# Row-wise argmax on one core: groups of four tiles, matching on GpSimd, five load buffers and a transposed result

## The chip, the core and the metric

The kernel runs on one core of a Trainium2 chip. A core has a matrix engine (TensorE, PE), VectorE (DVE), ScalarE (ACT), GpSimd (POOL) and SyncE (SP), which here only issues DMAs. Each engine works through its own instructions in order and they meet at semaphores. On-chip memory (SBUF) has 128 partitions; data comes from device memory over 16 DMA engines that all queues share. The metric is the device time of one execution in microseconds (us); lower is better.

## The reference

```python
def setup_inputs():
    return {"x": np.random.randn(8192, 8192).astype(np.float32)}

def reference(x):
    return np.argmax(x, axis=1)
```

For each of 8192 rows of 8192 floats, the position of the first maximum, as int64. The input is 268 MB and is read once in full; the output is 64 KB.

## The kernel before

The rows are worked in 64 tiles of 128 rows, one row per partition, so a tile is 4 MB. Each row is seen as C = 64 chunks of L = 128 elements. One loop over the tiles does all of the following for a tile before the next:

1. SP loads the tile into `xt` (L38).
2. VectorE reduces each chunk to its maximum, `chunkmax`, 128x64 (L41), the one instruction that reads the whole tile.
3. VectorE takes the eight largest of these (MAX8, L45; the row's maximum is the first) and the position of the maximum among the chunks, `cidx` (FIND_INDEX8, L46, with a load of the value to match ahead of it).
4. VectorE makes of it the number of the chunk in the input seen as (8192 x 64) chunks, `idx_full` (L49, L50).
5. POOL issues an indirect DMA, the gather (L54): it fetches for each row the one chunk that holds the maximum from device memory again, into `ga`, 128x128.
6. VectorE finds the maximum's position in that chunk, `lidx` (L62), and adds `cidx` x 128 (L67, L69) into the low word of `o`, whose high word ACT has cleared (L65).
7. SP stores `o`, 8 bytes per row (L71).

All tiles of SBUF come from pools with three buffers, so `xt` has three. The order on each engine is that of the loop: VectorE goes on to the next tile's reduce (L41) only after it has waited for this tile's gather at L62 and written `o` at L69. SP has one queue of issues with loads and stores in it: a load behind a store can be issued only when that store's wait for `o` is over. Index work on L67 doesn't need the gather and stands ahead of L62.

Of the kernel before, what the change touches and what calls it, by code (L numbers as in the profile page):

```python
# [1 line left out]

# [4 lines left out]


@with_exitstack
def kernel(  # L10
    ctx: ExitStack,
    tc: tile.TileContext,
    x: bass.AP,
    out: bass.AP,
):
    nc = tc.nc
    N, M = x.shape
    P = 128
    C = 64
    L = M // C  # L20
    ntiles = N // P

    pool = ctx.enter_context(tc.tile_pool(name="argmax_sbuf", bufs=3))
    opool = ctx.enter_context(tc.tile_pool(name="argmax_out", bufs=3))

    oth = out.tensor
    oth2 = type(oth)(name=oth.name, shape=[N, 2], dtype=mybir.dt.int32, base_partition=oth.base_partition)
    out_u32 = oth2.ap()

    x_flat = x.tensor.reshape([N * C, L]).ap()  # L30

    cpool = ctx.enter_context(tc.tile_pool(name="argmax_const", bufs=1))
    rowbase = cpool.tile([P, 1], mybir.dt.uint32)
    nc.gpsimd.iota(out=rowbase, pattern=[[1, 1]], base=0, channel_multiplier=C)  # L34

    for t in range(ntiles):
        xt = pool.tile([P, M], x.dtype)
        nc.sync.dma_start(out=xt[:, :], in_=x[t * P:(t + 1) * P, :])  # L38

        chunkmax = opool.tile([P, C], x.dtype)  # L40
        nc.vector.reduce_max(out=chunkmax, in_=xt.rearrange("p (c l) -> p c l", c=C), axis=mybir.AxisListType.X)  # L41

        mx8 = opool.tile([P, 8], x.dtype)
        cidx = opool.tile([P, 8], mybir.dt.uint32)
        nc.vector.max(out=mx8, in_=chunkmax)  # L45
        nc.vector.max_index(out=cidx, in_max=mx8, in_values=chunkmax)  # L46

        idx_full = opool.tile([P, 1], mybir.dt.uint32)
        nc.vector.tensor_tensor(out=idx_full, in0=cidx[:, 0:1], in1=rowbase, op=mybir.AluOpType.add)  # L49
        nc.vector.tensor_scalar(out=idx_full, in0=idx_full, scalar1=t * P * C, scalar2=None,  # L50
                                op0=mybir.AluOpType.add)

        ga = pool.tile([P, L], x.dtype)
        nc.gpsimd.indirect_dma_start(  # L54
            out=ga[:, :],
            out_offset=None,
            in_=x_flat[:, :],
            in_offset=bass.IndirectOffsetOnAxis(ap=idx_full[:, :1], axis=0),
        )

        lidx = opool.tile([P, 8], mybir.dt.uint32)
        nc.vector.max_index(out=lidx, in_max=mx8, in_values=ga)  # L62

        o = opool.tile([P, 2], mybir.dt.int32)
        nc.scalar.memzero(o[:, 1:2])  # L65
        tmp = opool.tile([P, 1], mybir.dt.uint32)
        nc.vector.tensor_scalar(out=tmp, in0=cidx[:, 0:1], scalar1=L, scalar2=None,  # L67
                                op0=mybir.AluOpType.mult)
        nc.vector.tensor_tensor(out=o[:, 0:1], in0=tmp, in1=lidx[:, 0:1], op=mybir.AluOpType.add)  # L69

        nc.sync.dma_start(out=out_u32[t * P:(t + 1) * P, :], in_=o[:, :])  # L71


# [1 line left out]
_INS = ['x']  # L75
_OUTS = [((8192,), 'int64')]


# [23 lines left out]
```

## Time and profile before

| | us |
|---|---|
| time, median of 3 runs | 1073.86 (1071.63 to 1075.15) |
| profiled execution: span from the first to the last instruction (no other time of it is recorded) | 1087.8 |
| VectorE busy | 639.6 |
| GpSimd busy | 60.8 |
| ScalarE busy | 14.0 |

The profile is of one execution of its own, under the hardware profiler, and its span is longer than the three timed runs. Its page has groups of instructions: line, engine, operation, the tiles written and read with their shapes, the count, then the busy time in us and the mean of one in ns, then the idle time of the engine just before these instructions and what ended that idle time. The 40 slices of the span show how evenly the work is spread. Digits are the busy share in tenths:

```profile
DVE  3657556465574664655656557556465574655756
POOL 0000000000000000000000000000000000000000
DMA  9888877787788777878787787887787878778760
GB/s 404 237 294 234 251 293 213 263 263 227 294 237 248 277 217 275 256 234 293 216 272 256 217 294 234 256 288 199 277 259 230 294 216 272 263 209 294 239 231 5
```

The first slice, when three loads are queued at the start, moves 404 GB/s; the others some 200 to 300. DMA share is the mean busy share of the 16 DMA engines.

### The profile page before, as it was taken

How to read it: one execution, taken by the hardware profiler on the slowest of the kernel's cores; microseconds unless marked ns; L12 is line 12 of the kernel's file. 1: busy time of each engine (PE TensorE's matmuls, PEld its weight loads, DVE VectorE, ACT ScalarE, POOL GpSimd, SP SyncE). 2: the span in 40 equal slices, each digit the busy share in tenths (PEclk: the TensorE clock that was granted, in tenths of full speed). 3: DMA queues.
4: the chain of work that ended last, by engine and by line, in shares of the span. 5: the costliest groups of instructions: out<-in, count | busy, mean ns of one | idle time of the engine just before them, and what ended most of it. 6: DMA issues, size and time to landing. Idle time of an engine off the chain costs nothing. (4 is left out here: it accounts for less than half of the span.)

```text
span 1087.8 us, 1198 instructions
## 1 busy us (share of the span) xinstructions
DVE 639.6 (59%) x640; ACT 14.0 (1%) x65; POOL 60.8 (6%) x69
## 2 busy tenths in 40 slices
DVE  3657556465574664655656557556465574655756
ACT  0000000000000000000000000000000000000000
POOL 0000000000000000000000000000000000000000
DMA  9888877787788777878787787887787878778760
GB/s 404 237 294 234 251 293 213 263 263 227 294 237 248 277 217 275 256 234 293 216 272 256 217 294 234 256 288 199 277 259 230 294 216 272 263 209 294 239 231 5
DMA packets 20489, 272.78 MB, mean 251 GB/s; under 512 B 11264, under 2 KB 11264, under 8 KB 12288
## 3 DMA queue, kind: packets, MB, share of 16 engines
q1 hardware_dynamic: 18432, 268.51, 76.6%
q0 software_dynamic: 2048, 4.20, 1.0%
q14 instruction: 9, 0.07, 0.0%
HBM read 272.63 MB, written 0.07 MB: 251 GB/s over the span
## 5 line engine op out<-in xcount | busy, mean ns | idle before, releaser
L41 DVE TENSOR_REDUCE chunkmax<-xt 128x64 f32<-128x8192 f32 x64 | 555.5, 8679 | 13.3 <-DMA xt<-in_x_dram 13.0
L62 DVE MATCH_VALUE_LOAD lidx<-mx,ga 128x8 f32 x64 | 5.9, 92 | 417.9 <-DMA ga<-in_x_dram,idx_full 417.9
L54 POOL DMA_INDIRECT ga<-in_x_dram,idx_full x64 | 60.5, 945 | 1019.4 <-DVE idx_full L50 1019.4
L65 ACT ACTIVATE o<-o 128x1 uint32<-128x1 uint32 x64 | 12.8, 202 | 1030.8 <-DMA out_dram<-o 1030.8
L62 DVE FIND_INDEX8 lidx<-mx,ga 128x8 uint32<-128x128 f32 x64 | 18.2, 285 | 0.0
L45 DVE MAX8 mx<-chunkmax 128x8 f32<-128x64 f32 x64 | 14.6, 228 | 2.2
L46 DVE FIND_INDEX8 cidx<-mx,chunkmax 128x8 uint32<-128x64 f32 x64 | 14.0, 219 | 0.0
L69 DVE TENSOR_TENSOR o<-tmp,lidx 128x1 int32<-128x1 uint32 x64 | 10.2, 159 | 6.0 <-issue 0.4
L49 DVE CUSTOM_DVE_ANT_0 idx_full<-cidx,rowbase 128x2 uint16<-128x2 uint16 x64 | 10.2, 159 | 2.3
L50 DVE TENSOR_SCALAR idx_full<-idx_full 128x1 uint32<-128x1 uint32 x64 | 9.8, 153 | 0.0
L67 DVE TENSOR_SCALAR tmp<-cidx 128x1 uint32<-128x1 uint32 x64 | 9.4, 147 | 0.0
L46 DVE MATCH_VALUE_LOAD cidx<-mx,chunkmax 128x8 f32 x64 | 5.9, 92 | 2.2
L65 ACT ACT_TABLE_LOAD x1 | 1.3, 1283 | 0.7 <-PEq L86 0.7
L34 POOL IOTA rowbase<- 128x1 uint32 x1 | 0.1, 118 | 0.4 <-PEq L97 0.4
L86 POOL MEMSET const-uint8-127<- 128x1 uint8 x1 | 0.1, 118 | 0.0
L86 POOL MEMSET const-bfloat16-1.0<- 128x1 bf16 x1 | 0.1, 113 | 0.0
L86 POOL MEMSET const-float32-0.0<- 128x1 f32 x1 | 0.1, 98 | 0.2 <-issue 0.2
L86 POOL MEMSET const-float32-1.0<- 128x1 f32 x1 | 0.1, 104 | 0.0
## 6 DMA issues: line engine op xcount, KB each, us to landing
xt<-in_x_dram SPq DMA_DIRECT2D x64, 4096.0 KB, 15.8
ga<-in_x_dram,idx_full POOLq DMA_INDIRECT x64, 6.3
out_dram<-o SPq DMA_DIRECT2D x64, 1.0 KB, 3.7
```

The source lines that it names most:

```text
L34: nc.gpsimd.iota(out=rowbase, pattern=[[1, 1]], base=0, channel_multiplier=C)
L41: nc.vector.reduce_max(out=chunkmax, in_=xt.rearrange("p (c l) -> p c l", c=C), axis=mybir.AxisListType.X)
L45: nc.vector.max(out=mx8, in_=chunkmax)
L46: nc.vector.max_index(out=cidx, in_max=mx8, in_values=chunkmax)
L49: nc.vector.tensor_tensor(out=idx_full, in0=cidx[:, 0:1], in1=rowbase, op=mybir.AluOpType.add)
L50: nc.vector.tensor_scalar(out=idx_full, in0=idx_full, scalar1=t * P * C, scalar2=None, op0=mybir.AluOpType.add)
L54: nc.gpsimd.indirect_dma_start(out=ga[:, :], out_offset=None, in_=x_flat[:, :], in_offset=bass.IndirectOffsetOnAxis(ap=idx_full[:, :1], ax ...
L62: nc.vector.max_index(out=lidx, in_max=mx8, in_values=ga)
L65: nc.scalar.memzero(o[:, 1:2])
L67: nc.vector.tensor_scalar(out=tmp, in0=cidx[:, 0:1], scalar1=L, scalar2=None, op0=mybir.AluOpType.mult)
L69: nc.vector.tensor_tensor(out=o[:, 0:1], in0=tmp, in1=lidx[:, 0:1], op=mybir.AluOpType.add)
L86: nc = _bacc.Bacc("TRN2", target_bir_lowering=False, num_devices=1)
```

## The change

The loop is rewritten. What it does now:

- **Loads.** `xt` has five buffers, and SP's queue holds nothing but loads until the end. The last tile is loaded in four parts and reduced in four.
- **Groups.** Tiles go in groups, fifteen of four, then two, one and one. The chunk maxima of a group lie in one tile `cm`, and one VectorE reduce (L93) gives the row maxima `mx` of the whole group.
- **Matching.** MAX8 and FIND_INDEX8 are gone. `first_match` does on POOL, per tile, an is-equal with the row's maximum and a product with descending weights (n, n-1, ..., 1); the largest product, taken by a VectorE reduce, tells the first match. It is used for the chunk (64 values) and, after the gather, within the chunk (128 values).
- **Stages.** After a group's last tile comes stage 2 (`mx`, matches of the chunks); one tile later stage 3 (`k`, `idx`, the group's gathers, matches in the chunks); three tiles after that stage 4 (`k2` and the result `res`). The list `pending` holds what is due. The calls wrapped in `keep` stay in the order in which they are written.
- **Result.** `res` holds one column per tile in float32. TensorE transposes 60 columns, and at the end the last four, against an identity matrix; ACT copies them as integers into the low words of `o`, whose high words were cleared by a POOL memset; SP stores whole rows of 128 results. There are two stores in place of 64.

The diff, cut to its core; the old loop, printed above, is removed whole:

```diff
-    pool = ctx.enter_context(tc.tile_pool(name="argmax_sbuf", bufs=3))
-    opool = ctx.enter_context(tc.tile_pool(name="argmax_out", bufs=3))
+    xpool = ctx.enter_context(tc.tile_pool(name="x_sbuf", bufs=5))
+    spool = ctx.enter_context(tc.tile_pool(name="small", bufs=3))
+    cpool = ctx.enter_context(tc.tile_pool(name="const", bufs=1))
+    ppool = ctx.enter_context(tc.tile_pool(name="psum", bufs=2, space=bass.MemoryType.PSUM))
...
+    descC = cpool.tile([P, C], F32)
+    nc.gpsimd.iota(out=descC, pattern=[[-1, C]], base=C, channel_multiplier=0,
+                   allow_small_or_imprecise_dtypes=True)
...
+    def first_match(vals, mx, desc, n, g, name):
+
+        w = spool.tile([P, g, n], F32, tag=f"w_{name}")
+        for i in range(g):
+            keep(nc.gpsimd.tensor_scalar(out=w[:, i, :], in0=vals[:, i, :], scalar1=mx[:, i:i + 1],
+                                    scalar2=None, op0=ALU.is_equal))
+            keep(nc.gpsimd.tensor_tensor(out=w[:, i, :], in0=w[:, i, :], in1=desc, op=ALU.mult))
+        k = spool.tile([P, g], F32, tag=f"k_{name}")
+        return w, k
+
+    groups = [4] * 15 + [2, 1, 1]
...
+    def run_due(now, all_=False):
+        while pending and (all_ or pending[0][0] <= now):
+            pending.pop(0)[1]()
+
+    def defer(due, fn):
+        pending.append((due, fn))
+        pending.sort(key=lambda e: e[0])
+
+    def store(t0, n):
+        ps = ppool.tile([n, P], F32, tag="ps")
+        nc.tensor.transpose(ps, res[:, t0:t0 + n], ident)
+        o = spool.tile([n, P, 2], I32, tag="o")
+        nc.gpsimd.memset(o, 0)
+        nc.scalar.copy(out=o[:, :, 0:1], in_=ps.unsqueeze(2))
+        keep(nc.sync.dma_start(out=out_i32[t0:t0 + n, :], in_=o.rearrange("t p two -> t (p two)")))
+
+    def stage2(t0, g, cm, now):
+        mx = spool.tile([P, g], F32, tag="mx")
+        keep(nc.vector.reduce_max(out=mx, in_=cm, axis=AX.X))
+        w, k = first_match(cm, mx, descC, C, g, "c")
+
+        def stage3():
+            keep(nc.vector.reduce_max(out=k, in_=w, axis=AX.X))
+            idx = spool.tile([P, g], U32, tag="idx")
+            keep(nc.vector.tensor_tensor(out=idx, in0=base[:, t0:t0 + g], in1=k, op=ALU.subtract))
+            ga = spool.tile([P, g, L], F32, tag="ga")
+            for i in range(g):
+                keep(nc.gpsimd.indirect_dma_start(
+                    out=ga[:, i, :], out_offset=None, in_=x_flat[:, :],
+                    in_offset=bass.IndirectOffsetOnAxis(ap=idx[:, i:i + 1], axis=0)))
+            w2, k2 = first_match(ga, mx, descL, L, g, "l")
+
+            def stage4():
+                keep(nc.vector.reduce_max(out=k2, in_=w2, axis=AX.X))
+
+                keep(nc.vector.scalar_tensor_tensor(out=res[:, t0:t0 + g], in0=k, scalar=float(L),
+                                               in1=k2, op0=ALU.mult, op1=ALU.add))
...
+                if t0 + g == 60:
+                    store(0, 60)
+
+            defer(now + 4, stage4)
+
+        defer(now + 1, stage3)
...
+            xt = xpool.tile([P, M], F32, tag="xt")
+            parts = 4 if t == NT - 1 else 1
+            w = M // parts
+            cw = C // parts
+            for q in range(parts):
+                keep(nc.sync.dma_start(out=xt[:, q * w:(q + 1) * w],
+                                  in_=x[t * P:(t + 1) * P, q * w:(q + 1) * w]))
+            for q in range(parts):
+                keep(nc.vector.reduce_max(
+                    out=cm[:, i, q * cw:(q + 1) * cw],
+                    in_=xt[:, q * w:(q + 1) * w].rearrange("p (c l) -> p c l", c=cw), axis=AX.X))
+            run_due(t)
+            t += 1
+        now = t - 1
+        stage2(t0, g, cm, now)
+    run_due(0, all_=True)
+    while pending:
+        run_due(0, all_=True)
+    store(60, NT - 60)
```

How this moves instructions on three engines. On VectorE, before, the second tile (DMAHW is the semaphore of a load, DMASW that of a gather, DVE and Pool those of the engines):

```order
L41 TENSOR_REDUCE chunkmax<-xt 128x64 [waits DMAHW1_49]
L45 MAX mx_91<-chunkmax 128x8 [waits DVE_49]
L46 MAX_INDEX cidx<-mx_91,chunkmax 128x8 [waits DVE_49]
L49 ISA idx_full<-cidx,rowbase 128x2 [waits DVE_49]
L67 TENSOR_SCALAR tmp<-cidx 128x1
L50 TENSOR_SCALAR idx_full<-idx_full 128x1 [waits DVE_49]
L62 MAX_INDEX lidx<-mx_91,ga 128x8 [waits DMASW1_49]
L69 TENSOR_TENSOR o<-tmp,lidx 128x1 [waits DVE_49]
```

On VectorE, changed, from stage 4 of the first group (after tile 7's reduce) to the reduce of tile 10 (`k<-w` at L108 is `k2` of the text, taken from the matches within the chunks; at L97 it is `k`, from the matches of the chunks):

```order
L108 TENSOR_REDUCE k<-w 128x4 [waits Pool_49]
L110 SCALAR_TENSOR_TENSOR res<-k 128x4 [waits DVE_49]
L112 TENSOR_SCALAR res<-res 128x4 [waits DVE_49]
L93 TENSOR_REDUCE mx<-cm 128x4
L135 TENSOR_REDUCE cm<-xt 128x64 [waits DMAHW0_49]
L97 TENSOR_REDUCE k<-w 128x4 [waits Pool_49]
L99 TENSOR_TENSOR idx<-base,k 128x4 [waits DVE_49]
L135 TENSOR_REDUCE cm<-xt 128x64 [waits DMAHW1_49]
L135 TENSOR_REDUCE cm<-xt 128x64 [waits DMAHW2_49]
```

VectorE's wait for a gather is gone; it waits for POOL twice a group instead, with a reduce or three between the cause and the wait.

On SP, before, from the start of the program:

```order
L38 DMA xt<-in_x_dram 128x8192 x3
L71 DMA out_dram<-o 128x2 [waits DVE_49,Activation_49]
L38 DMA xt<-in_x_dram 128x8192 [waits DMAHW0_49]
L71 DMA out_dram<-o 128x2 [waits DVE_49,Activation_49]
L38 DMA xt<-in_x_dram 128x8192 [waits DMAHW1_49]
```

On SP, changed, all of the program, without the waits (each load from the sixth on waits for the reduce that last read its buffer):

```order
L171 UNCONDITIONAL_BRANCH
L132 DMA xt<-in_x_dram 128x8192 x63
L132 DMA xt<-in_x_dram 128x2048 x4
L89 DMA out_dram<-o 60x256
L89 DMA out_dram<-o 4x256
```

Between two loads there stood a store that waited for the tile's result; now no store stands ahead of any load.

On POOL, changed, at the end of the program (the chunk matches, gather and in-chunk matches of tile 62, then of tile 63; before, POOL had only the 64 gathers):

```order
L63 TENSOR_SCALAR w<-cm,mx 128x64 [waits DVE_49]
L65 TENSOR_TENSOR w<-w,descC 128x64 [waits Pool_49]
L102 DMA ga<-in_x_dram,idx 128x128 [waits DVE_49]
L63 TENSOR_SCALAR w<-ga,mx 128x128 [waits DMASW6_49]
L65 TENSOR_TENSOR w<-w,descL 128x128 [waits Pool_49]
L63 TENSOR_SCALAR w<-cm,mx 128x64 [waits DVE_49]
L65 TENSOR_TENSOR w<-w,descC 128x64 [waits Pool_49]
L102 DMA ga<-in_x_dram,idx 128x128 [waits DVE_49]
L63 TENSOR_SCALAR w<-ga,mx 128x128 [waits DMASW7_49]
L65 TENSOR_TENSOR w<-w,descL 128x128 [waits Pool_49]
```

POOL's matches of tile 63's chunks now stand behind its wait for the gather of tile 62.

More of the change, by code (lines that the diff above doesn't have):

```diff
@@ L6 @@
 from concourse._compat import with_exitstack
+F32 = mybir.dt.float32
+U32 = mybir.dt.uint32
+I32 = mybir.dt.int32
+ALU = mybir.AluOpType
+AX = mybir.AxisListType
 @with_exitstack
@@ L28 @@
-    out_u32 = oth2.ap()
+    oth2 = type(oth)(name=oth.name, shape=[NT, 2 * P], dtype=I32, base_partition=oth.base_partition)
+    out_i32 = oth2.ap()
     x_flat = x.tensor.reshape([N * C, L]).ap()
[L32 to L71, printed above, removed]
@@ new lines @@
+    descC = cpool.tile([P, C], F32)
+    nc.gpsimd.iota(out=descC, pattern=[[-1, C]], base=C, channel_multiplier=0,
+                   allow_small_or_imprecise_dtypes=True)
+    descL = cpool.tile([P, L], F32)
+    nc.gpsimd.iota(out=descL, pattern=[[-1, L]], base=L, channel_multiplier=0,
+                   allow_small_or_imprecise_dtypes=True)
+    base = cpool.tile([P, NT], F32)
+    nc.gpsimd.iota(out=base, pattern=[[P * C, NT]], base=C, channel_multiplier=C,
+                   allow_small_or_imprecise_dtypes=True)
@@ new lines @@
+    ident = cpool.tile([P, P], F32)
+    nc.gpsimd.iota(out=ident, pattern=[[1, P]], base=0, channel_multiplier=-1,
+                   allow_small_or_imprecise_dtypes=True)
+    keep(nc.gpsimd.tensor_scalar(out=ident, in0=ident, scalar1=0.0, scalar2=None, op0=ALU.is_equal))
+    res = cpool.tile([P, NT], F32)
+    def first_match(vals, mx, desc, n, g, name):
[6 more added lines that the diff above has]
+        return w, k
@@ new lines @@
+    groups = [4] * 15 + [2, 1, 1]
+    assert sum(groups) == NT
+    pending = []
+    def run_due(now, all_=False):
[11 more added lines that the diff above has]
+        keep(nc.sync.dma_start(out=out_i32[t0:t0 + n, :], in_=o.rearrange("t p two -> t (p two)")))
@@ new lines, in stage2 @@
+    def stage2(t0, g, cm, now):
[16 more added lines that the diff above has]
+                                               in1=k2, op0=ALU.mult, op1=ALU.add))
+                keep(nc.vector.tensor_scalar(out=res[:, t0:t0 + g], in0=res[:, t0:t0 + g],
+                                        scalar1=-1.0, scalar2=float(C * L + L),
+                                        op0=ALU.mult, op1=ALU.add))
+                if t0 + g == 60:
+                    store(0, 60)
+            defer(now + 4, stage4)
+        defer(now + 1, stage3)
@@ new lines @@
+    t = 0
+    for g in groups:
+        cm = spool.tile([P, g, C], F32, tag="cm")
+        t0 = t
+        for i in range(g):
+            xt = xpool.tile([P, M], F32, tag="xt")
[13 more added lines that the diff above has]
+        stage2(t0, g, cm, now)
```

4 lines of the change are left out of this document (2 added, 2 removed).

## The prediction

> **What bounds the kernel now.** I read the page's groups first, for the busiest engine and the costliest wait (columns: line, engine, operation, tiles and count | busy us, mean ns of one | idle us just before, and what ended it).
>
> ```profile
> span 1087.8 us, 1198 instructions
> DVE 639.6 (59%) x640; ACT 14.0 (1%) x65; POOL 60.8 (6%) x69
> ...
> L41 DVE TENSOR_REDUCE chunkmax<-xt 128x64 f32<-128x8192 f32 x64 | 555.5, 8679 | 13.3 <-DMA xt<-in_x_dram 13.0
> L62 DVE MATCH_VALUE_LOAD lidx<-mx,ga 128x8 f32 x64 | 5.9, 92 | 417.9 <-DMA ga<-in_x_dram,idx_full 417.9
> L54 POOL DMA_INDIRECT ga<-in_x_dram,idx_full x64 | 60.5, 945 | 1019.4 <-DVE idx_full L50 1019.4
> ...
> L62 DVE FIND_INDEX8 lidx<-mx,ga 128x8 uint32<-128x128 f32 x64 | 18.2, 285 | 0.0
> L45 DVE MAX8 mx<-chunkmax 128x8 f32<-128x64 f32 x64 | 14.6, 228 | 2.2
> ```
>
> VectorE (DVE) is busy 59% of the span, and nearly all of its idle time, 417.9 us, is one wait: for the gather `ga`. It waits for a load only once, 13.0 us at the start; after that the large loads are always there in time. So the kernel is bound neither by arithmetic nor, as it stands, by bandwidth. The timeline of one steady tile shows the chain (columns: start us, duration us, engine, line, operation, idle before).
>
> ```profile
> 518.71 8.68 DVE L41 TENSOR_REDUCE chunkmax<-xt 128x64 f32<-128x8192 f32 x1
> 518.85 0.34 SPq L71 DMA_DIRECT2D out_dram<-o  x1
> 519.24 0.43 SPq L38 DMA_DIRECT2D xt<-in_x_dram  x1
> ...
> 528.09 0.15 DVE L67 TENSOR_SCALAR tmp<-cidx 128x1 uint32<-128x1 uint32 x1
> 528.21 0.15 DVE L50 TENSOR_SCALAR idx_full<-idx_full 128x1 uint32<-128x1 uint32 x1
> 528.63 0.94 POOL L54 DMA_INDIRECT ga<-in_x_dram,idx_full  x1 [15.54 <-DVE idx_full L50]
> 534.86 0.09 DVE L62 MATCH_VALUE_LOAD lidx<-mx,ga 128x8 f32 x1 [6.50 <-DMA ga<-in_x_dram,idx_full]
> ...
> 535.32 0.16 DVE L69 TENSOR_TENSOR o<-tmp,lidx 128x1 int32<-128x1 uint32 x1
> 535.39 8.68 DVE L41 TENSOR_REDUCE chunkmax<-xt 128x64 f32<-128x8192 f32 x1
> ```
>
> One period is 535.39 - 518.71 = 16.68 us: reduce 8.68, the index work up to 528.36 (0.97), the gather wait 6.50, the rest 0.53. Times 64 this is 1067.5 us, all but 20 us of the span. SP stands in the same chain: its store waits for `o`, and the next load behind it starts only then (519.24), although its buffer's reduce ended some 8 us before.
>
> What the loads could do otherwise is shown by the start, where three are queued at once. Stretches of the trace (columns: stretch, length, busy us and count by engine, clock, DMA share, GB/s), then the DMA queues' totals and the times from issue to landing of `xt` and `ga`:
>
> ```profile
> 13.00:22.50 9.50, 9.24 (x5) 0.00 (x0) 0.00 (x0) 1.00 1.02 442
> 13.00:25.00 12.00, 9.56 (x7) 0.00 (x0) 1.10 (x1) 1.00 1.01 437
> 22.50:31.00 8.50, 0.32 (x3) 0.00 (x0) 1.10 (x1) 1.00 1.01 436
> 1.90:32.40 30.50, 10.67 (x11) 0.51 (x4) 1.10 (x1) 1.00 0.95 407
> ...
> 200.00:1000.00 800.00, 478.52 (x477) 9.74 (x48) 44.58 (x48) 1.00 0.79 253
> ```
> ```profile
> q1 hardware_dynamic: 18432, 268.51, 76.6%
> q0 software_dynamic: 2048, 4.20, 1.0%
> ```
> ```profile
> DMA to landing us min/median/max: 12.3/15.8/31.0
> ```
> ```profile
> DMA to landing us min/median/max: 2.5/6.3/8.1
> ```
>
> With a queue, 437 GB/s at a full DMA share; with one load at a time, 253. A load alone lands after 15.8 us (median), though 4.194 MB at 437 GB/s is 9.6 us.
>
> **The change part by part.**
>
> *Gather wait leaves the chain.* `first_match` goes to GpSimd (POOL), and VectorE takes a group's results up one to four tiles later. VectorE then has per group of four: four reduces at 8.68 plus 0.03 of gap (34.8 us) and six small operations. Three are reduces over 256, 256 and 512 elements, at 8679/8192 = 1.06 ns each and about 0.06 fixed: 0.33 + 0.33 + 0.60. Three work on 128x4: 0.16 each by the rows of L69 and L50. With 0.3 for gaps between dependent ones that is 2.0 us, so **36.8 us a group, 9.2 a tile**, in place of 16.68. All MAX8 and FIND_INDEX8 work is gone.
>
> *Loads no longer stand behind stores.* SP has nothing but loads until the end, five in flight, each waiting for the reduce five tiles back. A fifth buffer over three costs nothing in time. At 437 GB/s one load is 9.60 us; the gathers take 1.0% of 1087.8 us over 64 tiles, 0.17 us each. **9.77 us a tile**, so loads, not VectorE, set the pace, by 39.1 against 36.8 us a group. A check: the three first loads are all issued within 1.3 us from 0.74; the last takes the 31.0 us, so it lands at 32 to 33, and two loads after the first (13.0) take 19 to 20, some 9.75 each.
>
> *What the waits added hide behind.* `k<-w` waits on POOL, whose eight chunk matches have the 8.68 us of one reduce as cover. Behind a late `k` stand the next three reduces and with them SP's loads. The trace of before has no such POOL operation: below stands POOL's 128x1 IOTA, 0.12 us; above POOL's longest row, the gather issue at 0.945. I take 0.4, nearest to VectorE's 0.285 for the same 128x128 plus that 0.12. Eight are 3.2 us (1.0 to 7.6): hidden at either end. The second pass, behind the gathers, has three tiles, 29 us, as cover: four issues at 0.945 (3.8), the landing at most 8.1, eight matches 3.2 (to 7.6): 15 to 20 us. Hidden. The group's POOL total is 3.8 + 8.1 + 6.4 = 18 us (to 27) of 39.
>
> A rule of the Trainium skill speaks against this part: GPSIMD Engine Reference, Engine selection, gives elementwise work to VectorE and calls GpSimd about twice as slow with two inputs. By the rows here VectorE has only 39.1 - 36.8 = 2.3 us a group to spare, while sixteen matches at its own 0.228 to 0.285 would be 4.1; POOL idles 1019.4 us. By the rule VectorE would set the pace at 40.9 us a group, by the trace's idle time GpSimd's slowness is free, so the sum doesn't take the rule.
>
> *Start and end.* The start stays at 13.0 us: the first load is issued as before, and the constants need only be ready four tiles later. The end is new. Its old rows:
>
> ```profile
> 1079.91 0.94 POOL L54 DMA_INDIRECT ga<-in_x_dram,idx_full  x1 [12.06 <-DVE idx_full L50]
> 1082.47 0.09 DVE L62 MATCH_VALUE_LOAD lidx<-mx,ga 128x8 f32 x1 [2.83 <-DMA ga<-in_x_dram,idx_full]
> 1082.55 0.28 DVE L62 FIND_INDEX8 lidx<-mx,ga 128x8 uint32<-128x128 f32 x1
> 1083.28 0.16 DVE L69 TENSOR_TENSOR o<-tmp,lidx 128x1 int32<-128x1 uint32 x1 [0.44 <-issue]
> 1083.50 0.33 SPq L71 DMA_DIRECT2D out_dram<-o  x1
> ```
>
> A gather in quiet costs 2.83 us; from the last VectorE result (1083.44) to the end are 4.4. The last load lands at 13.0 + 63 x 9.77 = **628.5**. Its four parts gain little, since tile 62's reduce (landed 618.7) and the small operations run until 628.2; four quarter reduces at 2.2 end at 637.0. Then, in series, because POOL's order puts tile 63's chunk match behind the gather of tile 62: five or six small VectorE operations (1.6), gather (2.8), four matches (1.6), `k` and `idx` (0.4), the second gather (2.8), two matches (0.8), three VectorE operations (0.6), transpose and copy (0.6 as an estimate: the copy by VectorE's and ACT's small rows of about 0.2, the transpose at the same with a hand-over; nothing to 2), store and end 4.4. That is 15.6; six matches at 0.12 or 0.945 make it 14 to 19. The large store of 60 rows goes out during this and is off the path.
>
> **Sum:** 637.0 + 15.6 = 653 us of span. The execution profiled before has a span of 1087.8 us against a median of 1073.86 in the runs shown, so 13.9 us (1.3%) more under the profiler. In its proportion 653 would be 645, taken off whole 639. I expect less of it here, as the DMA pace replaces a chain of instructions and waits, and take **650**, with 634 to 672 as its own range (pace 9.6 to 9.95, tail, this offset).
>
> **The rivals.**
>
> *VectorE takes the bound.* It has 2.3 us a group to spare. If its reduces stand still while POOL matches, sixteen at 0.29 or 0.4 add 4.6 to 6.4 us: 41.4 to 43.2 a group, 16 x that + 28 = 690 to 720; I put it at 700. For it: the two never ran such work together before. Against: the gather's issue by POOL at 0.945 moved no reduce, but that isn't the same work. 8%.
>
> *The memory doesn't hold its pace.* 437 GB/s is shown for some 20 us only. The mean over the first three loads, 407 GB/s with its slow start, would be 10.31 + 0.17 = 10.48 us a tile, 673 for the last landing and 698 in all. Against: 442 and 436 in the two stretches show no decline. 7%. The skill's DMA: Bandwidth & Descriptors, Where 436 GB/s comes from, says that the HBM side at about 358 GB/s binds such loads; by that figure a tile is an estimated 11.9 us and the whole near 787. The trace disagrees with it (437 for 12 us), and the skill's HBM Reference, Specifications, has a core streaming alone near 425.
>
> *Gathers stand behind the queued loads.* With four loads ahead of it a gather could land after 4 x 9.77 = 39 us; with 3.8 to issue and 3.2 to match that is 46 against 29 of cover. VectorE waits up to 17, but then the loads catch up and the next gather finds fewer ahead; so perhaps 5 us a group, 5 x 16 = 80: 730. Against: the first gather, issued while a load had ten microseconds to go, landed in 8.1, the maximum. 5%.
>
> *The overlap doesn't come*: the loads still go one at a time, 15.8 us and 0.4 to issue. 13.0 + 63 x 16.2 + 24 = 1058, faster by some 1.5%. Against: three were in flight at the start. 1%.
>
> *Slower: POOL becomes the chain.* Per group it does sixteen matches, 3.8 us of issues and a landing of 6.3, in order. Four tiles now take 66.7 us, so it decides from (66.7 - 10.1)/16 = 3.5 us a match; at 4.0 the group is 74.1, sixteen of them 1186, with start and end 1215. Every row of POOL here is at most 0.945. 2%.
>
> **How the numbers follow.** Forecast 77%, rivals 8, 7, 5, 1 and 2%. The range 634 to 702 takes in the forecast's own 634 to 672 and most of the first two rivals. What a measurement of this kernel can tell from no change is about 0.3%, 3 us; every case but the last is faster by more, save a sliver of the fourth: faster 0.97, same 0.01, slower 0.02.
>
> **What would show it.** Right: a DMA share near 1.0 and over 420 GB/s all through; VectorE's idle time before L135 waiting on `xt`, 0.4 to 0.6 us a tile; no more than a microsecond in all before `k<-w` (L97, L108) until the last group. Wrong: reduces longer than 8.68 us (first rival); loads spaced over 10 us with a full queue (second); long waits of L108 and gathers landing after 20 us or more (third); POOL matches over 1 us. Wrong, too, if the tail after the last reduce is far from 15.6 us.

## The result and the profile after

| | before | changed |
|---|---|---|
| time, median | 1072.74 us (1071.45 to 1075.15, 4 runs) | 667.04 us (666.91 to 667.11, 4 runs) |
| span of the profiled execution | 1087.8 us | 665.3 us |
| ratio | | 0.6217, 95% interval 0.6209 to 0.6226 |

The changed kernel takes 38% less time. The prediction said 650 us with a range of 634 to 702. The page of the changed kernel, its head, the two rows of slices and the costliest groups:

```profile
span 665.3 us, 723 instructions
...
PE 0.8 (0%) x2; PEld 0.2 (0%) x2; DVE 584.1 (88%) x175; ACT 1.8 (0%) x3; POOL 179.7 (27%) x331
...
DMA  9999999999999999999999999999999999999930
GB/s 378 441 428 425 424 441 426 426 431 420 439 426 428 426 426 440 423 430 420 430 423 442 431 418 430 425 440 418 430 431 426 439 421 430 428 426 439 405 161 12
...
DMA 76%; DVE 19%; issue 3%; POOL 0%; SPq 0%; POOLq 0%; PE 0%; ACT 0%; DVEq 0%; ACTq 0%
...
L135 DVE TENSOR_REDUCE cm<-xt 128x64 f32<-128x8192 f32 (+1 forms) x67 | 555.9, 8301 | 65.9 <-DMA xt<-in_x_dram 65.9
L63 POOL TENSOR_SCALAR w<-cm,mx 128x64 f32<-128x64 f32 x64 | 28.2, 441 | 261.4 <-DVE mx L93 261.4
L102 POOL DMA_INDIRECT ga<-in_x_dram,idx x64 | 62.4, 974 | 115.0 <-DVE idx L99 91.2
L63 POOL TENSOR_SCALAR w<-ga,mx 128x128 f32<-128x128 f32 x64 | 38.8, 606 | 91.7 <-DMA ga<-in_x_dram,idx 91.7
L65 POOL TENSOR_TENSOR w<-w,descL 128x128 f32<-128x128 f32 x64 | 29.1, 454 | 5.3
```

The DMA engines are busy at 0.9 or more until the last loads have landed, where before most slices stood at 0.7 to 0.9, and they move mostly 418 to 442 GB/s in place of some 200 to 300. The chain that ended last is now DMA for 76%, nearly all of it loads, while VectorE's largest wait has changed from `ga` (417.9 us) to `xt` (65.9 us, 13 of them the start). Waiting for the gather has moved to POOL (91.7 us), where it holds up nobody until the end of the kernel. The end of the kernel, from the timeline (start us, duration us, engine, line, operation, idle before):

```profile
630.11 8.69 DVE L135 TENSOR_REDUCE cm<-xt 128x64 f32<-128x8192 f32 x1 [2.05 <-DMA xt<-in_x_dram]
...
639.23 8.85 DVE L135 TENSOR_REDUCE cm<-xt 128x16 f32<-128x2048 f32 x4
...
649.93 1.05 POOL L102 DMA_INDIRECT ga<-in_x_dram,idx  x1 [4.57 <-DVE mx L93]
...
654.58 0.22 DVE L97 TENSOR_REDUCE k<-w 128x1 f32<-128x64 f32 x1 [4.80 <-POOL w L65]
...
655.27 1.04 POOL L102 DMA_INDIRECT ga<-in_x_dram,idx  x1 [0.73 <-DVE idx L99]
...
659.70 0.15 DVE L112 TENSOR_SCALAR res<-res 128x1 f32<-128x1 f32 x1
```

Tile 62 landed at 630.1 (its reduce starts on the landing), the last reduce ends at 648.1, and 17.2 us later the kernel ends, after two rounds of gather and match one behind the other.

### The profile page after: what moved, and what is told of

The parts are those of the page before. It is cut to its first block, busy times and chain, and to the rows that moved or that the text cites. A ratio compares the mean times of both kernels' runs of the same rounds, so it can differ in the third digit from the quotient of the medians.

```text
span 665.3 us, 723 instructions
## 1 busy us (share of the span) xinstructions
PE 0.8 (0%) x2; PEld 0.2 (0%) x2; DVE 584.1 (88%) x175; ACT 1.8 (0%) x3; POOL 179.7 (27%) x331
## 2 busy tenths in 40 slices
DMA packets 11786, 272.75 MB, mean 410 GB/s; under 512 B 2116, under 2 KB 2180, under 8 KB 3204
## 3 DMA queue, kind: packets, MB, share of 16 engines
q1 hardware_dynamic: 9731, 268.51, 94.5%
## 4 chain that ended last, share of the span: by engine, by line
DMA 76%; DVE 19%; issue 3%; POOL 0%; SPq 0%; POOLq 0%; PE 0%; ACT 0%; DVEq 0%; ACTq 0%
DMA xt<-in_x_dram 75%; DVE cm L135 18%; DMA ga<-in_x_dram,idx 1%; DVE k L108 0%; SPq L132 0%; POOL w L63 0%; DVE mx L93 0%; DVE k L97 0%; DVE res L110 0%; POOL w L65 0%; DVE res L112 0%; POOLq L171 0%; DVE idx L99 0%; PE ps L85 0%; ACT o L88 0%
## 5 line engine op out<-in xcount | busy, mean ns | idle before, releaser
L135 DVE TENSOR_REDUCE cm<-xt 128x64 f32<-128x8192 f32 (+1 forms) x67 | 555.9, 8301 | 65.9 <-DMA xt<-in_x_dram 65.9
L63 POOL TENSOR_SCALAR w<-cm,mx 128x64 f32<-128x64 f32 x64 | 28.2, 441 | 261.4 <-DVE mx L93 261.4
L102 POOL DMA_INDIRECT ga<-in_x_dram,idx x64 | 62.4, 974 | 115.0 <-DVE idx L99 91.2
L63 POOL TENSOR_SCALAR w<-ga,mx 128x128 f32<-128x128 f32 x64 | 38.8, 606 | 91.7 <-DMA ga<-in_x_dram,idx 91.7
L65 POOL TENSOR_TENSOR w<-w,descL 128x128 f32<-128x128 f32 x64 | 29.1, 454 | 5.3
L65 POOL TENSOR_TENSOR w<-w,descC 128x64 f32<-128x64 f32 x64 | 20.4, 319 | 5.3
L108 DVE TENSOR_REDUCE k<-w 128x4 f32<-128x512 f32 (+2 forms) x18 | 11.1, 617 | 2.9 <-POOL w L65 2.9
L97 DVE TENSOR_REDUCE k<-w 128x4 f32<-128x256 f32 (+2 forms) x18 | 6.8, 379 | 4.8 <-POOL w L65 4.8
L93 DVE TENSOR_REDUCE mx<-cm 128x4 f32<-128x256 f32 (+2 forms) x18 | 6.9, 382 | 0.1
L112 DVE TENSOR_SCALAR res<-res 128x4 f32<-128x4 f32 (+2 forms) x18 | 3.0, 168 | 0.6
```

The source lines that it names most:

```text
L63: keep(nc.gpsimd.tensor_scalar(out=w[:, i, :], in0=vals[:, i, :], scalar1=mx[:, i:i + 1], scalar2=None, op0=ALU.is_equal))
L65: keep(nc.gpsimd.tensor_tensor(out=w[:, i, :], in0=w[:, i, :], in1=desc, op=ALU.mult))
L93: keep(nc.vector.reduce_max(out=mx, in_=cm, axis=AX.X))
L97: keep(nc.vector.reduce_max(out=k, in_=w, axis=AX.X))
L102: keep(nc.gpsimd.indirect_dma_start(out=ga[:, i, :], out_offset=None, in_=x_flat[:, :], in_offset=bass.IndirectOffsetOnAxis(ap=idx[:, i:i ...
L108: keep(nc.vector.reduce_max(out=k2, in_=w2, axis=AX.X))
```

## The experiments

Twelve kernels, for three questions: which part of the change brings the gain, what sets the pace now, and can the end be moved. The kernel before was timed beside them on the same chips and took 1078 to 1081 us there, against 1072.74 beside the changed kernel. The changed kernel was not timed again on those chips. The kernel before differs between them by up to 8 us, so times alone don't show a difference of a few us from 667.04; where one is claimed below, rows of the traces say where it lies.

**1. The loads alone.** The kernel before, with five buffers and stores issued by ScalarE, so that no load stands behind a store.

```diff
-    pool = ctx.enter_context(tc.tile_pool(name="argmax_sbuf", bufs=3))
+    pool = ctx.enter_context(tc.tile_pool(name="argmax_sbuf", bufs=5))
...
-        nc.sync.dma_start(out=out_u32[t * P:(t + 1) * P, :], in_=o[:, :])
+        nc.scalar.dma_start(out=out_u32[t * P:(t + 1) * P, :], in_=o[:, :])
```

> The kernel before with five load buffers and its stores issued by ScalarE, so that no load stands behind a store; the gather stays in VectorE's chain. Theory (the serial gather is the bound): VectorE's period is still reduce 8.7, index work 1.3, gather 5 to 8.6, rest 0.5, so 16 to 19 us a tile and 1020 to 1220 us; only if the gather slips ahead of the next load is it 900 or more. Rival (loads behind stores were the bound): the loads run at 9.95 us a tile, 660 to 720 us.

Measured: 1149.58 us, ratio to before 1.063 (1.0603 to 1.0657). The group with VectorE's wait for the gather in this kernel, and from its timeline a load and the gather behind it:

```profile
L62 DVE MATCH_VALUE_LOAD lidx<-mx,ga 128x8 f32 x64 | 5.9, 92 | 478.8 <-DMA ga<-in_x_dram,idx_full 478.8
```
```profile
403.10 36.27 SPq L38 DMA_DIRECT2D xt<-in_x_dram  x3
...
404.32 0.94 POOL L54 DMA_INDIRECT ga<-in_x_dram,idx_full  x1 [17.21 <-DVE idx_full L50]
```

Freeing the loads alone makes the kernel slower. Each load now starts when a reduce ends, 1.2 us ahead of the gather that VectorE is about to wait for (before, some 9 us ahead), and the wait grows from 417.9 to 478.8 us. These 61 us are the whole difference between the spans of the two traces, 1148.8 and 1087.8; between the timed runs it is 68. The serial gather was the bound, as the prediction read it.

**2. The deferral alone.** The second match and the store of a tile are written behind the next tile's reduce; three buffers and stores on SP stay.

```diff
+        if late:
+            late.pop(0)()
         mx8 = opool.tile([P, 8], x.dtype)
...
+        def finish(t=t, mx8=mx8, cidx=cidx, ga=ga):
+            lidx = opool.tile([P, 8], mybir.dt.uint32)
+            keep(nc.vector.max_index(out=lidx, in_max=mx8, in_values=ga))
...
+        late.append(finish)
```

> The kernel before with the second match and the store of a tile moved behind the next tile's reduce; three buffers, stores on SP as before. Theory (both parts are needed): the gather wait goes, but each load is issued only after the store two tiles back, 10.7 us after the landing before; two loads then take 26.5 us, 13.3 us a tile, 800 to 870 us. Rival (the gather wait alone was the cost): VectorE's own work of 10.3 us a tile, 680 to 700 us.

Measured: 876.33 us, ratio 0.8103 (0.8084 to 0.8122): about half of the gain, and 6 us above the theory's 800 to 870. VectorE's waits (line, what it waited for, us in all, times, longest):

```profile
DVE chunkmax L43 <- DMA xt<-in_x_dram: 197.4, 61, 13.1
DVE lidx L67 <- DMA ga<-in_x_dram,idx_full: 23.1, 20, 4.7
```

The gather's wait is down to 23 us, and in its place VectorE waits 197 us for loads. Each load is still issued only behind a store that waits for VectorE's result, and lands 16.5 us later (median).

**3. Both together,** with VectorE's own matching, no groups and no transposed result: the edits of 1 and 2.

> Both of these together: second match one tile later, five buffers, stores issued by ScalarE; matching stays on VectorE, no groups, no transposed result. Theory: VectorE sets the pace with 8.7 + 1.5 us and a gather that lands about as late as the next reduce ends (0 to 1 us of wait), 10.3 to 11 us a tile, 675 to 725 us, my value 690. Rival (groups, GpSimd matching and whole-row stores carry much of the gain): over 750 us.

Measured: 856.74 us (849.51 to 858.79), ratio 0.791 (0.7865 to 0.7955). A miss by 130 us: the rival's number came out. VectorE's largest wait, the time from issue to landing of the stores (last column), rows of the timeline, and a stretch of 600 us with the DMA share and GB/s at its end:

```profile
DVE o L74 <- DMA out_dram<-o: 182.2, 51, 6.0
```
```profile
out_dram<-o ACTq DMA_DIRECT2D x64, 1.0 KB, 13.2
```
```profile
412.78 26.16 SPq L40 DMA_DIRECT2D xt<-in_x_dram  x3
...
416.15 0.20 ACT L70 ACTIVATE o<-o 128x1 uint32<-128x1 uint32 x1 [13.25 <-DMA out_dram<-o]
416.21 0.34 ACTq L76 DMA_DIRECT2D out_dram<-o  x1
416.24 0.16 DVE L74 TENSOR_TENSOR o<-tmp,lidx 128x1 int32<-128x1 uint32 x1 [3.17 <-DMA out_dram<-o]
```
```profile
200.00:800.00 600.00, 442.21 (x450) 9.12 (x45) 42.42 (x45) 1.00 0.96 320
```

A store of 128 times 8 bytes landed in 3.7 us before, where it was issued 0.4 us ahead of a load; here it is issued some 3 us behind one and takes 13.2. The clearing of `o` waits for the landing of an older store, the next store stands behind that clearing on ScalarE, and VectorE, which needs the cleared `o`, waits 182 us. So ScalarE's chain takes one landing a tile, and 64 x 13.2 = 845 us is nearly the whole time. My theory had given the stores no price. The stretch also shows that a DMA share near 1 doesn't mean full bandwidth: 0.96 stands here beside 320 GB/s.

**4. The same with a tile of `o` for each tile,** so that nothing waits for a store's landing.

```diff
+    zpool = ctx.enter_context(tc.tile_pool(name="argmax_o", bufs=64))
...
-            o = opool.tile([P, 2], mybir.dt.int32)
+            o = zpool.tile([P, 2], mybir.dt.int32)
```

> The kernel of the run with both parts (856.74 us), with a tile of o of its own for each of the 64 tiles, so that VectorE no longer waits until an old store of o has landed (182 us there). Theory (the 64 stores cost by their landing time alone, 13 us in the full queue, through the recycled o): 690 to 720 us. Rival (8192 writes of 8 bytes slow the loads themselves): loads 11 us or more apart, over 740 us.

Measured: 702.59 us (three runs at 702.46 to 702.64, one at 716.61), ratio 0.6509 (0.6492 to 0.6526), within the theory's range. But it stays 36 us above the changed kernel, because the loads themselves are slower, as the rival said, though not as much as its 11 us a load. A stretch of 500 us of this kernel, then of the changed one (columns: stretch, length, busy us and count by engine, clock, DMA share, GB/s):

```profile
100.00:600.00 500.00, 465.73 (x473) 0.00 (x0) 44.30 (x47) 1.00 1.01 405
```
```profile
100.00:600.00 500.00, 0.00 (x0) 0.00 (x0) 455.24 (x126) 0.00 (x0) 141.23 (x252) 1.00 1.00 428
```

Loads are 268.51 of some 272.75 MB, so 405 GB/s is 10.52 us a load and 428 is 9.95. The difference of 0.57 us over 63 loads is 36 us, the whole distance. VectorE is 93% busy here and has its 48 us of waiting for `xt`, so the loads still set the pace. The DMA queues (packets, MB, share of the span) of this kernel, loads and then stores, and the loads' queue of the changed one:

```profile
q1 hardware_dynamic: 9216, 268.44, 94.5%
q10 hardware_dynamic: 9216, 0.07, 0.7%
```
```profile
q1 hardware_dynamic: 9731, 268.51, 94.5%
```

The stores' own packets take 0.7% of 700.8 us, 5 us; the packets of the loads take 94.5%, 662 us here and 629 in the changed kernel. So the same loads run longer in the other kernel's company. That it is the 8-byte writes that stretch them is likely, but not shown: the gathers too come one by one here and not in fours, and the loads' rate rises from 392 GB/s (100 to 200 us) to 414 (400 to 500 us) with the same store in every tile. Of the 190 us between run 3 and the changed kernel, 154 are the waiting for landings of stores, which this run takes away; two whole-row stores avoid it. The cause of the other 36 is open.

**5. Three buffers** in the changed kernel (`bufs=5` to `bufs=3` on `xpool`).

> The changed kernel with three load buffers. Theory (one queued load behind the running one is enough): 667 to 680 us. Rival (five buffers are needed): the start of a load, some 5 us beyond its packets, shows again, 11 us or more a tile, over 720 us.

Measured: 667.22 us. The fourth and fifth buffer bring nothing that shows: the loads run at the same 428 GB/s from 100 to 600 us, and a load lands 21.1 us after its issue instead of 41.0, which only tells how long it stood in the queue.

**6. Half the reduce.** VectorE reads only 64 of each 128 elements.

```diff
-                    in_=xt[:, q * w:(q + 1) * w].rearrange("p (c l) -> p c l", c=cw), axis=AX.X))
+                    in_=xt[:, q * w:(q + 1) * w].rearrange("p (c l) -> p c l", c=cw)[:, :, 0:L // 2], axis=AX.X))
```

> The changed kernel with reduces over half of each chunk only (left out: the other 64 of each 128 elements), so VectorE has about 5 us a tile to spare. Theory (loads set the pace, and gathers stretch it): the landings keep 9.95 us, the end after the last landing shrinks by the reduce that is left behind, some 7 to 8 us: 658 to 661 us. Rival (VectorE's late release of buffers stretches two loads in four by 0.46 us): loads 9.71 apart throughout, 15 us less on top, 642 to 647 us.

Measured: 661.93 us, 5.1 less, about 1 us above what was expected. The same stretch, and the reduce of tile 62, which starts on its landing:

```profile
100.00:600.00 500.00, 0.00 (x0) 0.00 (x0) 242.16 (x123) 0.00 (x0) 138.44 (x250) 1.00 1.00 428
```
```profile
630.32 4.42 DVE L135 TENSOR_REDUCE cm<-xt 128x64 f32<-128x4096 f32 x1 [5.67 <-DMA xt<-in_x_dram]
```

VectorE's busy time falls from 455 to 242 us and the loads run at the same 428 GB/s. Tile 62 lands at 630.3, against 630.1 in the changed kernel. VectorE doesn't set the pace; the 5 us are the end alone.

**7. No gathers.** The 64 indirect DMAs are left out and the second pass reads a constant tile.

```diff
-            for i in range(g):
-                keep(nc.gpsimd.indirect_dma_start(
...
-            ga = spool.tile([P, g, L], F32, tag="ga")
+            ga = gfix
```

> The changed kernel without the 64 gathers (left out: the second pass runs on a constant tile instead of the fetched chunks). Theory (gathers stretch the loads by 0.92 us a group, and two stand in the tail at 2.6 us and a hand-over each): loads 9.69 apart, 15 us less, the tail 5 to 6 less: 645 to 649 us. Rival (VectorE sets the 9.95): only the tail's part, 661 to 663 us.

Measured: 643.88 us, 23.2 less and 1 us under the range on the theory's side. The stretch, and the last reduces:

```profile
100.00:600.00 500.00, 0.00 (x0) 0.00 (x0) 466.84 (x129) 0.00 (x0) 87.86 (x199) 1.00 1.00 432
```
```profile
627.50 6.66 DVE L133 TENSOR_REDUCE cm<-xt 128x16 f32<-128x2048 f32 x3
```

All 432 GB/s are loads now, 9.71 us each. So a gather stretches the loads by 9.95 - 9.71 = 0.24 us. In the trace the last reduce ends at 634.2 instead of 648.1: 13.9 us are the loads, 0.22 for each of the 62 between the first landing and that of tile 62. The other 9.3 us are the end, which has no gathers to wait for.

**8. Matching on VectorE,** the second pass at stage 4 (`nc.gpsimd.` to `nc.vector.` in `first_match`, and its call for `l` moved into `stage4`).

> The changed kernel with all matches on VectorE, the second pass at stage 4; POOL keeps the gathers alone. Theory: VectorE has 39.8 - 37.1 = 2.7 us a group to spare and gets sixteen operations of 0.15 to 0.29, 2.4 to 4.6 with their gaps, so it comes to the loads' pace or just over it: 39.8 to 41.7 us a group, and the tail is shorter by some 2 us (fewer hand-overs): 663 to 697 us, my value 672. Rival (GpSimd's part is what made the gain): over 700 us.

Measured: 671.32 us, as expected and 4.3 slower than on GpSimd. VectorE's matches in this kernel, and its last reduces:

```profile
L63 DVE TENSOR_SCALAR w<-ga,mx 128x128 f32<-128x128 f32 x64 | 17.9, 279 | 0.0
L63 DVE TENSOR_SCALAR w<-cm,mx 128x64 f32<-128x64 f32 x64 | 16.0, 250 | 0.6
```
```profile
648.19 8.86 DVE L134 TENSOR_REDUCE cm<-xt 128x16 f32<-128x2048 f32 x4
```

An is-equal over 128 takes VectorE 279 ns and GpSimd 606, yet GpSimd's version is faster: VectorE waits only 18.6 us for `xt` here, 13.2 of them at the start, so it is at its limit, and GpSimd has time. The last reduce ends at 657.1 instead of 648.1, 9 us later; the end behind it is 5 us shorter. Moving the matches to GpSimd is worth the difference of some 4 us and no more.

**9 and 10. The end.** In 9, what is due at tile 63 runs after the first of its quarter reduces (`if t == NT - 1 and q == 0: run_due(t)` in the reduce loop). In 10, besides, tiles 48 to 61 come in halves and 62 and 63 in quarters (`parts = 4 if t >= NT - 2 else 2 if t >= NT - 16 else 1`).

> The changed kernel with what is due at tile 63 (results of group 14, index and gather of tile 62) run after the first of tile 63's four quarter reduces instead of after the last. Theory (the tail is a serial chain with two gather rounds, because POOL's order puts tile 63's chunk match behind tile 62's gather): one round, 2.6 us of landing and 1 to 2 us of matches less, the moved VectorE work neutral: 662 to 664 us, my value 663.3. Rival (the end is set by landing and store alone): 667 us, no change.

> The same, and tiles 48 to 61 loaded and reduced in halves, 62 and 63 in quarters, so that VectorE starts on a tile before it has landed whole. Theory (VectorE needs 9.2 us a tile against 9.95 between landings, but always starts a whole tile late): it catches up about 0.65 us a tile, until only a half or a quarter is left behind the last landing at 640: the end comes 4 to 6 us earlier than in the run before: 657 to 659.5 us. Rival (smaller loads lose on the DMA what VectorE gains): 662 us or more.

Measured: 666.19 and 665.01 us; both fall short. Rows of the second up to where VectorE takes up `k` of tile 62:

```profile
641.09 0.62 POOL L63 TENSOR_SCALAR w<-ga,mx 128x128 f32<-128x128 f32 x1 [3.30 <-DMA ga<-in_x_dram,idx]
...
643.50 0.44 POOL L63 TENSOR_SCALAR w<-cm,mx 128x64 f32<-128x64 f32 x1
...
644.38 0.22 DVE L97 TENSOR_REDUCE k<-w 128x1 f32<-128x64 f32 x1 [5.85 <-POOL w L65]
```

The reduces did come earlier: the quarters of tile 63 start at 635.3 instead of 639.2. But `k` now stands between them, and its chunk match on POOL is queued behind POOL's wait for the gather of tiles 60 and 61. VectorE waits 5.85 us (2.81 in run 9) with three quarter reduces behind it. An instruction moved ahead in one engine's order met the other engine's old order.

**11. Chunks of 64 elements** (`C = 64` to `C = 128`), so that a gather fetches 256 bytes a row.

> The changed kernel with 128 chunks of 64 elements per row in place of 64 of 128, so that a gather fetches 256 bytes a row instead of 512; POOL's two passes swap sizes, VectorE gets 0.27 us a group more. Theory A (a gather costs the loads by its bytes, 0.22 us a tile): half of 14 us, 659 to 662 us. Theory B (it costs by its 128 pieces): 666 to 669 us, no gain.

Measured: 662.47 us, 4.6 less: between the theories, 0.5 us outside A's range. The gathers' share of the DMA time falls too (changed kernel, then this one):

```profile
q0 software_dynamic: 2048, 4.20, 1.7%
```
```profile
q0 software_dynamic: 2048, 2.10, 1.0%
```

Tile 62 lands at 625.9 in this trace, 4.2 us earlier than in the changed kernel. By bytes alone half of the 13.9 us of run 7 would have gone, 7; so only part of what a gather costs the loads goes with its bytes.

**12. Combined:** chunks of 64, halves and quarters, tiles 60 to 62 as one group, and the due work after the second quarter reduce.

```diff
-    C = 64
+    C = 128
...
-    groups = [4] * 15 + [2, 1, 1]
+    groups = [4] * 15 + [3, 1]
...
-            parts = 4 if t == NT - 1 else 1
+            parts = 4 if t >= NT - 2 else 2 if t >= NT - 16 else 1
...
+                if t == NT - 1 and q == 1:
+                    run_due(t)
```

> A combined version: 128 chunks of 64, tiles 48 to 61 in halves and 62 and 63 in quarters, the last groups three tiles and one, and what is due at tile 63 run after its second quarter reduce. Theory (in the two tail runs VectorE stood 2.8 and 5.9 us before k of tile 62, because POOL had that tile's chunk match behind the gather of tiles 60 and 61; with 60 to 62 in one group POOL has nothing ahead of it): no wait of VectorE for POOL over 1 us before the last reduce, one gather round behind it, 653 to 658 us. Rival (the end can't be moved, only the loads' pace): 661 to 663 us, as with the 64-element chunks alone.

Measured: 656.03 us (655.83 to 656.55, 5 runs), ratio to before 0.6084 (0.6074 to 0.6093), 11 us less than the changed kernel. VectorE's only waits for POOL are the two of the one round behind the last reduce:

```profile
DVE k L108 <- POOL w L65: 3.1, 1, 3.1
DVE k L97 <- POOL w L65: 2.8, 1, 2.8
```

## Why the prediction was right, and where its sizes were off

- **What bound the kernel before.** Right, by runs 1 and 2: with the loads freed and the chain kept, 1149.58 us; with the chain cut and the loads kept, 876.33. Neither part reaches the result without the other, and by runs 3 and 4 both together do not reach it either while 64 small stores stay. What the groups of four give by themselves was not tried apart.
- **Loads set the pace, not VectorE.** Right, by runs 6 and 7. The term was mis-sized: 9.77 us a tile became 9.95. The load alone takes 9.71 us and not 9.60, because 437 GB/s read from a stretch of 12 us is 432 over 500 us; and a gather costs 0.24 us (0.22 by the landings) and not the 0.17 that its packets' share of the DMA time gave. Times 62 the 0.18 us are 11.2: tile 62 landed at 630.1, forecast at 618.7. VectorE's wait for `xt` behind the start is 52.9 us, 0.84 a tile and not 0.4 to 0.6, mostly for the same reason.
- **VectorE's 36.8 us a group.** Close: the small reduces take 0.41, 0.41 and 0.68 in place of 0.33, 0.33 and 0.60. The fixed 0.06 us taken for each stands in no row of before; by 407 ns for 256 elements and 676 for 512 it is some 0.14.
- **POOL's matches are hidden.** Right: 0.32 to 0.61 us each, in the bounds of 0.12 and 0.945, and VectorE waits for them twice, both times in the tail (4.8 and 2.9 us).
- **The end.** The four parts of the last tile gained little, as said: their reduces start at 639.2, about 1 us before the whole tile would have landed (630.1 and one load's 9.95), and take 8.85 us together. No run leaves the parts out. The tail of 15.6 us measured 17.2, with its two gather rounds as forecast from POOL's order.
- **From span to time.** The step "I expect less of it here", 653 to 650, went the wrong way: the profiled run of the changed kernel took 667.03 us with its span of 665.3, and in run 1 the same pair is 1150.58 and 1148.8. The time stands 1.7 to 1.8 us above the span. The span of 1087.8 then means that the profiled execution of before was itself a slower one than the runs shown, and nothing was to be taken off. Pace, tail and this step erred in the same direction, 17 us in all; none made up for another, and the time stays in the forecast's own 634 to 672.
- **What was not priced.** The step "loads no longer stand behind stores" counted only the order on SP. Runs 3 and 4 show that 64 small stores cost 154 us where engines wait for their landings. In run 4, with that waiting gone, the loads still take 36 us more than in the changed kernel; that the stores cause this too is not shown.
- **The rivals.** VectorE's reduces beside POOL's matches take 8683 ns (8679 before): none of the first. 428 GB/s held for 500 us: none of the second. The figure of about 358 GB/s of the Trainium skill (DMA: Bandwidth & Descriptors, Where 436 GB/s comes from) doesn't hold for this core alone. Gathers landed in 8.6 us (median; 10.7 at most) with four loads queued: none of the third. The loads overlap, 41.0 us from issue to landing at 9.95 apart, and POOL's matches take at most 0.62 us: none of the last two. The rule of the Trainium skill that elementwise work belongs on VectorE (GPSIMD Engine Reference, Engine selection) fits the single operations, 293 ns against 454 for the product over 128, and not the kernel, by the 4.3 us of run 8.

## What to carry to other kernels

Before freeing a queue, see which engine waits in series: with the chain left in place, loads that started as soon as a buffer was free only delayed the small transfer that the chain waited for. Beside a stream of loads a small transfer can have two prices, a longer landing for whoever waits on it (13.2 us in place of 3.7 for a store) and a stretch of the stream itself (0.24 us for a gather); the profile of before, with mostly one load under way, showed little of either. Read the share of busy DMA engines together with the GB/s. And when work is moved ahead on one in-order engine, check what stands before its supplier on the other one.

## What the runs showed that I had not expected

- 128 writes of 8 bytes land in 3.7 us when issued just ahead of a load, in 13.2 some 3 us behind one on the other queue, and in 16.1 with four loads queued. In that last kernel the loads run at 405 GB/s in place of 428.
- One queued load behind the running one is enough here: three buffers give 667.22 us, five 667.04.
- Halving a gather's bytes took some 4 of the 14 us that the gathers cost the loads, not half.
- On GpSimd the is-equal with one tile as input (441 ns over 64, 606 over 128) is slower than the product of two tiles (319 and 454).
